# Weight sums one every second step over four chunks, Fourier weights requested by ACT's queue, last residuals in tiles of their own, first position a step later

## The chip, the cores and the metric

The kernel runs on one core of one Trainium2 chip. The metric is the device time of one execution, in microseconds (us). Each time is the median of several runs.

## The reference

The trunk has two layers over two sequences, a prompt of 2048 tokens and a sample of 512, with 1024 channels. All arithmetic is float32.

```python
def attention_layer(x, g, w_in, w_out, sink, rel_bias):
    h = rmsnorm(x, g)
    z = h @ w_in                                  # q, k, v, gate
    ...
    o = banded_gqa_with_sink(q, k, v, rel_bias, sink)   # |i-j| <= 128, 16 heads, 4 kv heads
    return x + (o * jax.nn.silu(gate)) @ w_out

def fourier_layer(x, g, w_gate, w_out):
    h = rmsnorm(x, g)
    hg = h.astype(jnp.float32).reshape(b, s, N_FGROUPS, FGROUP_CH)   # 4 groups of 256 channels
    f = jnp.fft.fftn(hg, axes=(1, 3), norm="ortho").real             # over positions and group channels
    gate = h @ w_gate
    return x + (f.reshape(b, s, d) * jax.nn.silu(gate)) @ w_out

# y = rmsnorm(fourier_layer(attention_layer(x, ...), ...), final_norm), for the prompt and for the sample
```

## The kernel before

Every matmul runs on float32 operands that are split in a high part (rounded to the type fp32r) and a low part (the rest). `matmul3` (L85) issues three matmuls for a product, high by high, high by low and low by high: these are lines L87, L88 and L89, and most of TensorE's work stands in them.

**Attention phase** (`attention_phase`, L120). The tokens are taken in five chunks of 512 (`CHUNKS`, L37): chunk 0 is the sample, chunks 1 to 4 are the prompt. In a chunk, keys and values come first (`kv_proj`), then a loop of 64 positions and a few more for the lag (L564 on, `for i in range(64 + LAG + AVLAG)`). A position is one head pair `p`, one block of 128 queries `b` and one head `j`. At each position the loop issues

- the scores (`scores`, L383): TensorE L389 into a PSUM bank `spt`; DVE L401 adds the bias and finds the maximum, which releases the bank; ACT L405 takes the exponential; DVE L410 divides;
- three positions later the transposes (`transp`, L413): TensorE L421, ACT L422 casts the high part `pts`, DVE L423 takes the low part;
- two positions after that the products with the values (`av`, L435) and their evacuation (`out_evac`, L440, with GpSimd L450 and L453);
- between these, `fill`: the projections of the next head pair, or in the last eighth the output projection (`out_proj`, L457).

The output projection's `evac` (L474) loads the residual `xr` by SyncE (L479), DVE adds the projection (L480), and SyncE stores the sum to `x1d` (L481), the input of the second layer. The tag "xr" has three buffers. The steps of the last chunk's output projection that do not fit in the loop are returned as `tail` and run at the start of the Fourier phase (L846).

**Weight sums.** The gate product of the Fourier layer is done by a scheme with seven products in place of eight. It needs sums of quarters of `w_gate`: B11, T1, T2, B22, T3, N4 and B21. They are made during the attention phase, and go to DRAM (`sumd`) as high and low parts. `gate_sums(k)` (L502) makes the sums of one of four parts in ten steps: a load of two tiles `w32g`, seven `kept` steps and two steps of GpSimd arithmetic (`sums`, `more`). `fout_parts` (L527) splits the output weights in the same way into `foutd`, eight times a load (`w32f`) and two `kept` steps. A `kept` step is `keep` (L495):

```python
                t = ap.tile([P, 2, 512], F32R, tag="x", bufs=4, name="kept")
                ACT.copy(t[:, 0], src)
                pieces(t[:, 1], src, f32(t[:, 0]), ALU.subtract)
                POOL.dma_start(f32(dst), f32(t))
```

The two GpSimd instructions of `pieces` are L493. Loaded and kept tiles share the tag "x" with four buffers. `EXTRA` gives the steps to the chunks, and L590 to L593 issue one at each of the positions 4 to 27.

**Fourier phase** (`fourier_phase`, L619). The 20 tiles of 128 tokens are taken in ten pairs, 17 and 16 first. For a pair, `norms` (L692, with `norm` L673 and `sumsq` L667) loads the tiles of `x1d` and normalises them; the square of `sumsq` (ACT L670) writes to a junk tile of the tag "xr". `turn` (L695) transposes the tiles: TensorE `trb` L701, ACT `tTb` L703, DVE L704 for the low part. `sums` and `parts` make the sums of the transposed tiles. `z` (L725) is the transform over the channels of a group, and `gates` (L759) the seven products. These are accumulated in the PSUM tiles W, Z and X: first W with B11, then X step 0 with B21, Z with T1, W with T2, X step 1, Z with B22, W with T3, X steps 2 and 3, and W with N4. The weights B11 to N4 are loaded once, by `load_sums` (L816, GpSimd L820), four tiles of 512 KB each; those of B21 are streamed through `more` (L751, SyncE). `hook(i)` runs work between the products: the next pair's transposes, sums and `z`. At each second pair `combine` (L875) takes the four tiles' transforms together and stores them (`gsd`, `evd`, `odd`).

The loop over the tail (L846) issues the norms of the first pair (its tiles are loaded by ACT's queue) after tail steps 2 and 4, and the loads of B11, T1, T2 and B22 after step 5.

Then the transform over the positions: `position` (L907) takes the transforms `gl` of the sample (loaded from `gsd` by `sample`, L1005), casts them to `gs` on ACT (L931) and multiplies with the tables into the PSUM tiles As and Bs; the product with the gates `s2` gives `u`. `split_T` (L648) transposes `u` (`tru`, TensorE L655), and `finish` (L959) does the output projection `fo` with the 16 weight tiles `wo` (from `foutd`, loaded by GpSimd), adds the residual x2 and takes the final norm. The first position, of the sample's tiles 2 and 3, is run inside the last pair's gates, at hook 0; the others follow in `step`.

A framework places the instructions: each engine has one queue in order, semaphores between queues are set by the tiles that instructions share, and a tile of a pool waits until the earlier user of its buffer is done.

Of the kernel before, what the change touches and what calls it, by code (L numbers as in the profile page):

```python
# [18 lines left out]
P = 128  # L19
# [25 lines left out]
def encoder(  # L45
# [64 lines left out]
            (SP if lo_engine else POOL).dma_start(f32(wsd[n]), f32(w))  # L110
        return w[:, 0], w[:, 1]

    stage = []

    def after(ins, anchor):

# [3 lines left out]
    def attention_phase():  # L120

        with ExitStack() as es:
# [334 lines left out]
            def out_proj(c, uTs):  # L457
                tok = CHUNKS[c][0]
                steps = []
                st = {}  # L460

                def mm(half, k):
                    if k == 0:
                        st["ps"] = [bank(f"op{c}_{half}_{i}") for i in range(4)]
                    if k % 2 == 0:
                        st["w"] = load_w(c, 20 + half * 4 + k // 2, f"o{c}_{half}_{k}")
                    hi, lo = st["w"]
                    ws = slice((k % 2) * 512, (k % 2) * 512 + 512)
                    for i in range(4):
                        cs = slice(i * P, (i + 1) * P)  # L470
                        a = (uTs[k][0][:, cs], uTs[k][1][:, cs])
                        matmul3(st["ps"][i], a, (hi[:, ws], lo[:, ws]), k == 0, k == KD - 1)

                def evac(half):  # L474
                    for i in range(4):
                        rows = slice(tok + i * P, tok + (i + 1) * P)
                        cols = slice(half * 512, half * 512 + 512)
                        xt = main.tile([P, 512], F32, tag="xr", bufs=3, name=f"xr{c}_{half}_{i}")
                        SP.dma_start(xt, x[rows, cols])  # L479
                        DVE.tensor_tensor(xt, xt, st["ps"][i], ALU.add)  # L480
                        SP.dma_start(x1d[rows, cols], xt)  # L481

                for half in range(2):
                    for k in range(KD):
                        steps.append(lambda half=half, k=k: mm(half, k))
                    steps.append(lambda half=half: evac(half))
                return steps
# [36 lines left out]
                return [load, kept("B11", "B11"), kept("B22", "B22"), kept("B21", "B21"), sums, kept("T3", "B22"),  # L524
                        kept("T1", "B12"), more, kept("T2", "B11"), kept("N4", "B21")]

            def fout_parts(half, k2):  # L527
                st = []

                def load():  # L530
                    st.append(ap.tile([P, 2, 512], F32, tag="x", bufs=4, name=f"w32f{half}_{k2}"))
                    after(SP.dma_start(st[0].rearrange("p k c -> p (k c)"), w_fout[half, k2]), last_exp[0])

                return [load] + [lambda kk=kk: keep(foutd[half * 8 + k2 * 2 + kk], st[0][:, kk]) for kk in range(2)]

            EXTRA = {1: [gate_sums(0), gate_sums(1)], 2: [gate_sums(2), gate_sums(3)],
                     3: [fout_parts(h, k2) for h in range(2) for k2 in range(4)]}

            HB = [(b, j) for b in range(4) for j in range(2)]
            tail = []  # L540
# [6 lines left out]
            for c in range(len(CHUNKS)):  # L547
# [19 lines left out]
                for i in range(64 + LAG + AVLAG):  # L567
                    p, n = divmod(i, 8)
                    if n == 0 and i < 64:
                        if p < 7:  # L570

                            fill = qg_proj(c, p + 1, hs, res[p + 1], invb0)
                            fill.pop(0)()
                            at[p + 1][0]()
                            if i == 0 and c == 0:

                                for s in fill[:8]:
                                    s()
                                fill = fill[8:]
                        else:  # L580
                            op = out_proj(c, uTs)
                            fill, rest, tail = op[:4], op[4:7], op[7:]
                    if c + 1 < len(CHUNKS):
                        if i == 24:
                            norm_steps = stats(c + 1)
                        if i >= 28 and i % 4 == 0 and norm_steps:
                            inv = norm_steps.pop(0)()
                        elif i == 56:
                            invb = spread(c + 1, inv)
                    if i == 3:  # L590
                        extra = [s for steps in EXTRA.get(c, []) for s in steps]
                    if 4 <= i < 28 and extra:
                        extra.pop(0)()  # L593
                    if c == 0 and i % 8 == 3 and 1 <= p < 7:
                        load_w(0, LATE[p - 1], f"late{p}", late=last_exp[0])
                    if i < 64:
                        at[p][1](*HB[n])
                    k = i - LAG
                    if 0 <= k < 64:
                        at[k // 8][2](*HB[k % 8])  # L600
                    if i < 64:
                        m = len(fill) * (n + 1) // 8 - len(fill) * n // 8
                        todo = fill[len(fill) * n // 8 :][:m]
                        for s in todo[: m // 2]:
                            s()
                    k -= AVLAG
                    if 0 <= k < 64 and k % 2 == 1:
                        b = k % 8 // 2
                        at[k // 8][3](b)
                        if b % 2 == 1:  # L610
                            at[k // 8][4](b)
                    if i < 64:
                        for s in todo[m // 2 :]:
                            s()
                    elif rest:
                        rest.pop(0)()
            return tail

    def fourier_phase(tail):  # L619
        with ExitStack() as es:  # L620
# [1 line left out]
            psum2 = es.enter_context(tc.tile_pool(name="psum2", bufs=2, space=PSUM, reuse_waits="tile"))  # L622

            gb = fp.tile([P, D], F32, tag="gb", bufs=1, name="g1b")
            SP.dma_start(gb, bass.AP(g1.tensor, g1.offset, [[0, P], [1, D]]))
            mir = fp.tile([P, 8], I32, name="mir")
            SP.dma_start(mir, mirror)


            def left(shape, dtype, name):  # L630
# [35 lines left out]

            def sumsq(src, name):  # L667
                ss = main.tile([P, 8], F32, tag="ss", bufs=2, name=f"ss{name}")
                junk = main.tile([P, 512], F32, tag="xr", bufs=3, name=f"jk{name}").bitcast(BF16)
                ACT.activation(junk, src, AF.Square, accum_out=ss[:, 0:1])  # L670
                return inv_rms(ss, 1, f"inv{name}")

            def norm(t, queue=SP):  # L673

                xt = left([P, D], F32, f"x1_{t}")
                queue.dma_start(xt, x1d[t * P : (t + 1) * P, :])
                inv = sumsq(xt, f"b{t}")
                DVE.scalar_tensor_tensor(xt, xt, inv[:, 0:1], gb, ALU.mult, ALU.mult)
                return xt

# [4 lines left out]
            class Pair:  # L687
# [1 line left out]
                    self.n, self.ts, self.x, self.ps, self.A, self.F, self.S = n, ts, [None, None], {}, {}, {}, {}  # L689
                    self.zs = [None, None]  # L690

                def norms(self, i, queue=SP):  # L692
                    self.x[i] = norm(self.ts[i], queue)

                def turn(self, i, hf):  # L695

# [119 lines left out]
            def load_sums(place, *names):  # L816
                for w in names:
                    for k in range(4):
                        t = place([P, 2, 512], F32R, f"w{w}_{k}")
                        POOL.dma_start(f32(t), f32(sumd[w][k]))  # L820
                        wg[w][k] = (t[:, 0], t[:, 1])

            def tt(out, a, b, op):
# [21 lines left out]
            pairs = [Pair(2 * gi + i // 2, tiles[i : i + 2]) for gi, tiles in enumerate(order) for i in (0, 2)]  # L845
            for i, s in enumerate(tail):  # L846
                s()
                if i in (2, 4):
                    pairs[0].norms((4 - i) // 2, ACT)
                if i == 5:  # L850
                    load_sums(left, "B11", "T1", "T2", "B22")
            wstack.close()
            zp = es.enter_context(tc.tile_pool(name="zp", bufs=1, side="right", reuse_waits="tile"))

# [37 lines left out]
            for n, pr in enumerate(pairs[:-1]):  # L892
                nx = pairs[n + 1]
                for i in range(2):
                    nx.norms(1 - i)
                gates(pr, {
                    1: [lambda: turns1(nx)], 2: [lambda: turns2(nx)], 3: [lambda: turns3(nx)], 4: [lambda: turns4(nx)],
                    5: [lambda: nx.z(1, 0), lambda: nx.z(1, 1)],
                    6: [lambda: nx.z(0, 0), lambda: nx.z(0, 1), lambda: combine(nx)],
                })  # L900
# [58 lines left out]
            def finish(uT, r, last=False):  # L959
# [2 lines left out]
                out = rows(dst, (r0 - off, r[1]))  # L962
                if last:
                    ss = main.tile([P, 8], F32, tag="ss", bufs=2, name="ssl")
                    junk = main.tile([P, 512], F32, tag="xr", bufs=3, name="jkl").bitcast(BF16)
                x2 = x_tile(f"x2_{r0}")
                SP.dma_start(x2, rows(x1d, r))
                for half in range(2):
# [36 lines left out]
            def sample(k1, ids):  # L1005
                gl = []
                for i in ids:
                    g = zt(f"gl{i}")
                    SP.dma_start(g, gsd[i])
                    gl.append(g)  # L1010
                return f"s{k1}", 4 * k1, gl[0], gl[1] if len(gl) > 1 else None, pair(k1, 4, SEQ)

            first = []
            gates(pairs[-1], {0: [lambda: first.extend(position(*sample(1, (2, 3))))]})
            wo = []
            for k in range(16):
                t = left([P, 2, 512], F32R, f"wo{k}")
# [171 lines left out]
```

## Time and profile before

| | |
|---|---|
| Median of 3 runs | 1752.29 us (1750.26 to 1753.46) |
| Profiled execution | 1751.27 us |
| Its span in the profile | 1749.5 us |
| Mean granted TensorE clock | 0.985 |
| TensorE busy | 1667.1 us, 95% of the span |
| DVE, ACT, GpSimd busy | 1190.6, 857.7, 440.9 us |
| Bytes moved by DMA | 380.35 MB, 217 GB/s in the mean |

The profile is one execution. A line such as "PE spt L389 <- DVE S L401" in the chain of waits says that TensorE's instruction of line L389, which writes tile `spt`, waited for DVE's instruction of line L401 on tile `S`; the numbers behind it are the us in total, the number of waits and the longest one. In the profile PE is TensorE, POOL is GpSimd and SP is SyncE; "kept<-w32g" is an instruction that reads `w32g` and writes `kept`. The granted clock is the share of full speed that TensorE was allowed. The stages in the trace: chunk 0 ends at about 245 us, chunk 1 at 490, chunk 2 at 735, chunk 3 at 950, chunk 4 at 1183; the gates run to 1473 and the positions and the output projection to the end.

### The profile page before, as it was taken

To read this page: it belongs to the slowest core of one execution; us is meant where nothing else is said; L and a number is where in the kernel's file an instruction comes from. 1 tells how busy PE (TensorE), PEld (TensorE's weight loads), DVE (VectorE), ACT (ScalarE), POOL (GpSimd) and SP (SyncE) were. 2 spreads that over 40 slices of the span, in tenths; PEclk is the share of its full clock that TensorE was granted. 3 is DMA by queue.
4 is the path that set the end of the run, shared out by engine and by line. 5 is a ranking of instruction groups with operands and counts; after the bars stand their busy time and mean duration, and the time that the engine had idled before them with its cause. 6 is when DMAs were issued, how large, how long until landed. Compare 5 with 4: busy or idle time off the path is not lost. (4 is left out here: it accounts for less than half of the span.)

```text
span 1749.5 us, 25848 instructions
## 1 busy us (share of the span) xinstructions
PE 1667.1 (95%) x8980; PEld 1422.5 (81%) x8980; DVE 1190.6 (68%) x2774; ACT 857.7 (49%) x1966; POOL 440.9 (25%) x599
## 2 busy tenths in 40 slices
PE   9999899899989899999999999998999998999998
PEld 6878678688887788887888888887888887788886
DVE  5898654788538887457785388835777665888553
ACT  6678533576325575236664166624555543343221
POOL 2467732721305511305313011121000001112000
PEclk9999999899999999999999999998999999999999
DMA  8477776655576554668644843378665559763431
GB/s 303 173 285 302 271 282 234 228 181 196 183 258 244 211 193 148 222 253 283 236 171 164 315 139 125 129 272 353 223 223 181 191 194 405 281 234 111 146 106 49
DMA packets 104638, 380.35 MB, mean 217 GB/s; under 512 B 12171, under 2 KB 22411, under 8 KB 86588
## 3 DMA queue, kind: packets, MB, share of 16 engines
q1 hardware_dynamic: 84924, 294.54, 47.8%
q0 software_dynamic: 19152, 82.85, 12.0%
q8 instruction: 72, 1.18, 0.3%
q10 hardware_dynamic: 432, 1.31, 0.2%
q14 instruction: 58, 0.48, 0.1%
HBM read 284.25 MB, written 94.40 MB: 216 GB/s over the span
## 5 line engine op out<-in xcount | busy, mean ns | idle before, releaser
L405 ACT ACTIVATE S<-S 128x385 f32<-128x385 f32 (+1 forms) x320 | 191.1, 597 | 79.1 <-DVE S L401 78.4
L423 DVE TENSOR_TENSOR pts<-pt,pts 128x384 fp32r<-128x384 f32 (+1 forms) x320 | 168.4, 526 | 48.8 <-ACT pts L422 46.8
L389 PE MATMUL spt<-kwin,qab 128*128 128x384 f32 (+1 forms) x640 | 162.5, 336 | 31.7 <-DVE S L401 31.5
L401 DVE CUSTOM_DVE_ANT_0 S<-spt,b 128x385 f32<-128x385 f32 (+1 forms) x320 | 168.4, 527 | 28.0 <-PE spt L389 24.0
L410 DVE TENSOR_SCALAR S<-S 128x384 f32<-128x384 f32 (+1 forms) x320 | 174.1, 544 | 8.9
L422 ACT CAST pts<-pt 128x384 fp32r<-128x384 f32 (+1 forms) x320 | 143.8, 451 | 71.5 <-PE pt L421 68.2
L389 PEld LDWEIGHTS spt<-kwin,qab 128*128 128x128 f32 x640 | 117.3, 190 | 67.9 <-DVE S L401 44.2
L450 POOL TENSOR_TENSOR o<-o,s 128x256 f32<-128x256 f32 x75 | 55.2, 736 | 416.1 <-DVE o L446 409.7
L421 PE MATMUL pt<-ident,S 128*128 128x128 f32 x896 | 151.5, 275 | 1.4 <-ACT S L405 0.8
L435 PEld LDWEIGHTS av<-pts,v 128*128 128x128 f32 x896 | 128.4, 192 | 15.4 <-DVE pts L423 3.0
L435 PE MATMUL av<-pts,v 128*128 128x256 f32 x896 | 137.3, 287 | 2.3 <-DVE pts L423 2.2
L87 PE MATMUL gp<-h,wg 128*128 128x512 f32 x320 | 139.2, 435 | 0.0
L87 PE MATMUL qp<-h,wq 128*128 128x512 f32 x320 | 137.3, 429 | 0.6 <-ACT wq L101 0.6
L87 PE MATMUL op<-wo,uT 128*128 128x512 f32 x320 | 126.8, 399 | 2.9 <-DVE xr L480 2.8
L421 PEld LDWEIGHTS pt<-ident,S 128*128 128x128 f32 x896 | 114.5, 141 | 17.8 <-DVE pts L423 4.3
L89 PE MATMUL gp<-h,wg 128*128 128x512 f32 x320 | 127.1, 397 | 0.0
L87 PE MATMUL fo<-wo,tTu 128*128 128x512 f32 x320 | 125.9, 393 | 1.2 <-DVE x L973 1.2
L88 PE MATMUL gp<-h,wg 128*128 128x512 f32 x320 | 126.8, 396 | 0.0
L89 PE MATMUL qp<-h,wq 128*128 128x512 f32 x320 | 126.2, 394 | 0.1
L88 PE MATMUL op<-wo,uT 128*128 128x512 f32 x320 | 126.1, 394 | 0.0
L88 PE MATMUL qp<-h,wq 128*128 128x512 f32 x320 | 125.6, 393 | 0.0
L89 PE MATMUL op<-wo,uT 128*128 128x512 f32 x320 | 125.4, 394 | 0.0
(326 smaller groups left out, 4133.5 us busy)
## 6 DMA issues: line engine op xcount, KB each, us to landing
wq<-wsd SPq DMA_DIRECT2D x32, 1024.0 KB, 4.9
wg<-wsd SPq DMA_DIRECT2D x32, 1024.0 KB, 6.8
wo<-wsd SPq DMA_DIRECT2D x32, 1024.0 KB, 4.8
b<-B21d SPq DMA_DIRECT2D x40, 512.0 KB, 5.0
x<-x1d SPq DMA_DIRECT2D x38, 512.0 KB, 4.3
b<-rowd SPq DMA_DIRECT2D x40, 384.0 KB, 4.4
xs<-in_x_dram SPq DMA_DIRECT2D x23, 512.0 KB, 7.1
xr<-in_x_dram SPq DMA_DIRECT2D x40, 256.0 KB, 5.7
```

Source lines behind the costliest of these rows:

```text
L87: PE.matmul(out, a[0], b[0], start=start, stop=False, skip_group_check=more)
L88: PE.matmul(out, a[0], b[1], start=False, stop=False, skip_group_check=more)
L89: PE.matmul(out, a[1], b[0], start=False, stop=stop, skip_group_check=more)
L389: PE.matmul(ps[:, 2 + k0 * P : 2 + k1 * P], q, kwin[g][:, part, b * P + k0 * P : b * P + k1 * P], start=part == 0, stop=part == 1,)
L401: DVE.tensor_tensor_reduce(out=s[:, e0:e1], in0=ps[:, 1 + e0 : 1 + e1], in1=st["bias"][:, j, 386 - e1 : 386 - e0][:, ::-1], scale=1.0, sca ...
L405: last_exp[0] = ACT.activation(s[:, e0:e1], s[:, e0:e1], AF.Exp, bias=mn, scale=-1.0, accum_out=den)
L410: DVE.tensor_scalar(s[:, ks], s[:, ks], den, None, ALU.mult)
L421: PE.transpose(ps[:, kb, :], s[:, 1 + kb * P : 1 + (kb + 1) * P], ident)
L422: ACT.copy(hi[:, k0:k1, j, :], ps[:, k0:k1, :])
L423: DVE.tensor_tensor(lo[:, k0:k1, j, :], ps[:, k0:k1, :], f32(hi[:, k0:k1, j, :]), ALU.subtract)
L435: PE.matmul(out, v, pt[:, kb].rearrange("p h q -> p (h q)"), start=kb == k0 and part == 0, stop=kb == k1 - 1 and part == 1,)
L450: eng.tensor_tensor(of, of, res["s"][:, cs], ALU.mult)
```

## The change

It has six edits.

1. `EXTRA` gives one `gate_sums` to each of chunks 1 to 4, and the fout parts follow the last of them in chunk 4. A step is issued at each even position from 4 on, up to 27 (up to 59 in chunk 4). `fout_parts` loads the next tile with each first part.
2. The loads of B11 to N4 are issued by ACT in place of GpSimd, those of B11 and T1 after tail step 1, those of T2 and B22 after step 4.
3. The loads of the first pair's tiles and of `g1b` are issued after tail step 1, by ACT, apart from the norms. For the other pairs each load still stands right before its norm.
4. The residual tiles `xr` of the tail's last `evac` are allocated apart, each in a place of its own (`res_tile`).
5. The junk tile of the squares takes the tag "c12" (one buffer, shared with the gates' `c12`) in place of "xr". The load of `mir` moves from the start of the Fourier phase to the point before the last gates, on GpSimd.
6. The first position's `gl` tiles are allocated as `x_tile` and requested before the last gates, and the position runs at hook 4 in place of hook 0.

```diff
-    stage = []
+    stage, res_tile = [], []
 ...
-                        xt = main.tile([P, 512], F32, tag="xr", bufs=3, name=f"xr{c}_{half}_{i}")
+                        if res_tile:
+                            xt = res_tile[0](f"xr{c}_{half}_{i}")
+                        else:
+                            xt = main.tile([P, 512], F32, tag="xr", bufs=3, name=f"xr{c}_{half}_{i}")
 ...
-            def fout_parts(half, k2):
+            def fout_parts():
                 st = []
                 def load():
-                    st.append(ap.tile([P, 2, 512], F32, tag="x", bufs=4, name=f"w32f{half}_{k2}"))
-                    after(SP.dma_start(st[0].rearrange("p k c -> p (k c)"), w_fout[half, k2]), last_exp[0])
-                return [load] + [lambda kk=kk: keep(foutd[half * 8 + k2 * 2 + kk], st[0][:, kk]) for kk in range(2)]
-            EXTRA = {1: [gate_sums(0), gate_sums(1)], 2: [gate_sums(2), gate_sums(3)],
-                     3: [fout_parts(h, k2) for h in range(2) for k2 in range(4)]}
+                    n = len(st)
+                    if n < 8:
+                        st.append(ap.tile([P, 2, 512], F32, tag="x", bufs=4, name=f"w32f{n}"))
+                        dst = st[n].rearrange("p k c -> p (k c)")
+                        after(SP.dma_start(dst, w_fout[n // 4, n % 4]), last_exp[0])
+                def part(n, kk):
+                    if kk == 0:
+                        load()
+                    keep(foutd[n * 2 + kk], st[n][:, kk])
+                return [load] + [lambda n=n, kk=kk: part(n, kk) for n in range(8) for kk in range(2)]
+            EXTRA = {1: gate_sums(0), 2: gate_sums(1), 3: gate_sums(2), 4: gate_sums(3) + fout_parts()}
 ...
-                    if i == 3:
-                        extra = [s for steps in EXTRA.get(c, []) for s in steps]
-                    if 4 <= i < 28 and extra:
-                        extra.pop(0)()
+                    if 4 <= i < (60 if c == 4 else 28) and i % 2 == 0 and EXTRA.get(c):
+                        EXTRA[c].pop(0)()
 ...
             gb = fp.tile([P, D], F32, tag="gb", bufs=1, name="g1b")
-            SP.dma_start(gb, bass.AP(g1.tensor, g1.offset, [[0, P], [1, D]]))
             mir = fp.tile([P, 8], I32, name="mir")
-            SP.dma_start(mir, mirror)
 ...
-                junk = main.tile([P, 512], F32, tag="xr", bufs=3, name=f"jk{name}").bitcast(BF16)
+                junk = fp.tile([P, 512], F32, tag="c12", bufs=1, name=f"jk{name}").bitcast(BF16)
 ...
-                        POOL.dma_start(f32(t), f32(sumd[w][k]))
+                        ACT.dma_start(f32(t), f32(sumd[w][k]))
 ...
             for i, s in enumerate(tail):
                 s()
+                if i == 1:
+                    res_tile.append(lambda name: left([P, 512], F32, name))
+                    for k in range(2):
+                        pairs[0].load(1 - k, ACT)
+                    ACT.dma_start(gb, bass.AP(g1.tensor, g1.offset, [[0, P], [1, D]]))
+                    load_sums(left, "B11", "T1")
                 if i in (2, 4):
-                    pairs[0].norms((4 - i) // 2, ACT)
-                if i == 5:
-                    load_sums(left, "B11", "T1", "T2", "B22")
+                    pairs[0].norms((4 - i) // 2)
+                if i == 4:
+                    load_sums(left, "T2", "B22")
 ...
                 for i in range(2):
+                    nx.load(1 - i)
                     nx.norms(1 - i)
 ...
                 for i in ids:
-                    g = zt(f"gl{i}")
+                    g = x_tile(f"gl{i}")
                     SP.dma_start(g, gsd[i])
 ...
+            POOL.dma_start(mir, mirror)
             first = []
-            gates(pairs[-1], {0: [lambda: first.extend(position(*sample(1, (2, 3))))]})
+            one = sample(1, (2, 3))
+            gates(pairs[-1], {4: [lambda: first.extend(position(*one))]})
```

## The prediction

> **What bounds the kernel now.** I read the page's busy times first, then what TensorE waits for, then those waits window by window.
>
> ```profile
> PE 1667.1 (95%) x8980; PEld 1422.5 (81%) x8980; DVE 1190.6 (68%) x2774; ACT 857.7 (49%) x1966; POOL 440.9 (25%) x599
> ```
>
> TensorE is the bound: 1749.5 - 1667.1 = 82 us without matmul is all that better scheduling can win. The chain of waits, for TensorE:
>
> ```profile
> PE spt L389 <- DVE S L401: 31.5, 20, 3.5
> PE As L87 <- ACT gs L931: 7.7, 1, 7.7
> PE z L87 <- DVE xr L480: 7.6, 1, 7.6
> ```
>
> So 46.8 us of the 82 are three kinds of wait: scores waiting for a PSUM bank that L401 still reads, one wait before the first Fourier position, one at the start of the Fourier phase. The windows (columns: window, length, busy us of PE, PEld, DVE, ACT, POOL with counts, granted clock, DMA share, GB/s) give the place and the clock that each wait costs afterwards:
>
> ```profile
> 294.00:326.00 32.00, 27.84 (x149) 23.37 (x149) 26.68 (x64) 18.61 (x46) 22.64 (x33) 0.95 0.71 253
> 326.00:352.00 26.00, 20.76 (x105) 17.48 (x104) 17.77 (x46) 13.66 (x35) 19.96 (x30) 0.87 0.58 206
> 542.00:568.00 26.00, 22.69 (x124) 18.40 (x123) 22.97 (x49) 14.82 (x36) 18.41 (x27) 1.00 0.73 257
> 568.00:594.00 26.00, 20.29 (x95) 16.54 (x94) 20.78 (x44) 13.58 (x33) 21.32 (x32) 0.87 0.59 218
> 798.00:846.00 48.00, 42.58 (x237) 35.17 (x236) 34.30 (x99) 30.60 (x76) 26.79 (x40) 1.00 0.78 277
> 950.00:1147.00 197.00, 197.00 (x1106) 172.10 (x1105) 139.30 (x409) 101.15 (x258) 26.62 (x32) 1.00 0.51 178
> 1187.00:1196.00 9.00, 1.39 (x7) 0.92 (x6) 1.31 (x3) 0.03 (x1) 2.64 (x5) 0.70 1.03 415
> 1196.00:1201.00 5.00, 5.00 (x25) 5.00 (x25) 4.41 (x7) 2.83 (x5) 1.05 (x2) 0.51 1.03 419
> 1463.00:1468.00 5.00, 5.00 (x20) 4.48 (x20) 3.43 (x8) 2.80 (x9) 1.05 (x2) 0.59 1.03 421
> ```
>
> The first five rows are the four weight-sum sets (two in chunk 1, two in chunk 2) and the fout parts (chunk 3). Chunk 4, the sixth row, has no such steps and no idle TensorE. What the sums do is seen in the timelines of ACT, DVE and GpSimd (start, duration, idle before and its releaser):
>
> ```profile
> 335.52 0.62 ACT L498 CAST kept<-w32g 128x512 fp32r<-128x512 f32 x1 [4.68 <-DMA B11d<-kept]
> 1168.86 0.57 POOL L82 TENSOR_TENSOR invb<-invb,mhalf 128x1 f32<-128x1 f32 x1 [12.44 <-DMA mir<-in_mirror_dram]
> 1194.65 0.69 DVE L480 TENSOR_TENSOR xr<-xr,op 128x512 f32<-128x512 f32 x1 [7.96 <-DMA xr<-in_x_dram]
> 1462.04 1.66 ACT L931 CAST gs<-gl 128x512 fp32r<-128x512 f32 x3 [11.79 <-DMA gl<-gsd]
> ```
>
> At 335.52 the `kept` copy is the head of ACT's queue and waits until an earlier kept store frees one of the four "x" tiles. The exp and the pts cast behind it wait too, then DVE, then the scores. That is the mechanism of the 31.5 us.
>
> **Part 1, the weight sums.** Idle plus clock loss ((1 - clock) x length) per set: 4.2 + 1.6 = 5.8; 5.2 + 3.4 = 8.6; 3.3 + 0; 5.7 + 3.4 = 9.1; fout parts 5.4. Sum 32.2 us. The work itself stays: 44 kept copies (28 of w32g, 16 of w32f) at 0.62 us on ACT, their 88 pieces at 0.74 us on GpSimd, 44 stores.
>
> The source says one step every second position. The instruction order that both kernels are built to says otherwise for a set: in chunk 1 ACT has the seven kept copies between the same exps before and after, about one per position. So I don't count the halved pace as a gain for the sets. What does change is that a set no longer follows another directly, finding its "x" tiles still held: the second sets (8.6 and 9.1) are the dear ones, the first sets cost 5.8 and 3.3. After, there are four first sets: 5.8 in chunk 1, 3.3 in chunk 2, and for chunks 3 and 4 the mean, 4.5 each: 18.1. The fout parts do spread: in chunk 4 their copies come as a pair every four positions, with the load one step ahead. Before, they came at about twice that pace and cost 5.4. I take 1.5, nearer to zero since chunk 4 had 197.00 of 197.00 busy and carries no next chunk's norms. After: 19.6. **Gain 32.2 - 19.6 = 13 us.** Ends: the chunk 3 and 4 steps are free (9.1 left: gain 23), or each set costs today's mean of 6.7 and fout stays at 5.4 (32.2: gain 0).
>
> The granted clock weighs here: in 294:326 the longest single wait is 2.6 us and the clock still fell to 0.95, so I charge clock to shorter waits as well. The Trainium skill ("TensorE: Matmul & The Clock Gate", Part 1: The HAM clock gate) says that the clock halves after at least one idle window of about 3.4 us; by it first sets would cost idle alone, 1.6 us less in chunk 1; the trace disagrees for this one.
>
> **Part 2, the start of the Fourier phase.** Before, TensorE waits 7.61 us (to 1195.39) and then runs 5.5 us at half clock (2.7 lost): 10.4 us. The chain: the residual load xr4_1_3 is issued at 1187.75, when the store of the tile whose buffer it takes over has landed; it lands at 1194.57; DVE's L480 waits for it with the transposed tiles' parts queued behind; z17_1 waits for those. GpSimd issues B11_0 and B11_1 at 1155.4, is then held by invb until 1169.4, and issues the rest until 1197.8.
>
> After, the residuals have tiles of their own, so that wait is gone, but another stands in its place: in the built order SP's and ACT's transfers share eight completion lanes, each issue waiting for the transfer eight earlier, and the four xr4_1 loads wait for T2_0 to T2_3 to land. ACT issues g1b, two x1 tiles, then 16 weight tiles, 512 KB each, from about 1161.5. DMA is saturated from 1165 (1.03, 415 GB/s): 0.524 MB take 1.26 us. Up to T2_3 that is 15 tiles, 19 us, plus the last attention weights and stores: landed at about 1183 to 1188, so xr4_1_3 lands at about 1190 to 1194, sharing with B22. z17_1 starts at about 1193 instead of 1195.4.
>
> Behind it: T3_0 and T3_1 on ACT wait for B22_0 and B22_3 (about 1191 and 1196), and tTb16, which z16 needs, is queued behind T3_1. All z of the pair now precede W0, so no W covers the wait, as it did before (L87 W at 1186.24). X0 needs b21_0, which landed at 1208.7 before and can't be sooner: the bytes are the same and DMA is full until 1210. So I expect about 6 idle at z17_1, 3 at z16, 1 later, and 2.4 of clock: 12.4. **Loss 2 us.** Ends: -10 (all waits covered) and +8 (z16 at 1203).
>
> The 24 requests leave GpSimd (0.53 us each) for ACT (0.33 to 0.6 each, by the few ACT issues there are); the first 11, about 5 us, lie in a stretch where ACT is busy 2.1 to 2.5 us of each window of 7 to 15. What moving them wins is the 13.5 us in which GpSimd was held, and DMA's slack in 1150:1165, share 0.79, that is 3 us. The Trainium skill ("Trainium Kernel Development and Optimization", Key Constraints) says that requests from several queues run on the same 16 DMA engines and save only issue time; the share of 1.03 agrees, and without that rule the end of -10 would be nearer.
>
> **Part 3, the gates.** From 1210 to 1450 TensorE has no gap over 0.5 us. The junk tile of sumsq now shares the single c12 buffer, so each square waits for the gate product that reads c12, and the next c12 copy for it; ACT and DVE have room. I take 0; ends -1 and +4 (eight norms at 0.5).
>
> **Part 4, the first position.** Before, its second gl load sat in SP's queue behind the odd and evd stores (issued at 1451.07, gs copied at 1462.04). TensorE idles 7.7 us from 1455.02, then runs 4.4 us at half clock (the 0.59 row): 9.9 us. After, both gl loads are issued before the last gates and the position runs at hook 4, four products later; this wait goes. What is late next: the 16 wo tiles, requested by GpSimd, landed from 1448.1 to 1479.5 with DMA at 1.02 and more, then s2s (1487.1) and x2 (1489.6). fo began at 1474.18; it would now be ready at about 1465, when wo7 (1465.7) has just landed, and its second half needs wo15. The gl loads (1 MB, 2.5 us) are out of that stretch. I return 4 of 9.9. **Gain 6 us;** ends 0 (wo sets the end) and 10.
>
> **The rest**, 1500 to 1749: the built order barely moves; 0.
>
> **Sum.** -13 + 2 + 0 - 6 = -17 us. The profiled run took 1751.27 (span 1749.5 and 1.8 around it): 1734.3. The median is 1.0 above that run: **1735 us.**
>
> **Rivals.**
> (a) *The sums' stalls only move* (the edit doesn't do what it says): the order of copies in a set is unchanged, which speaks for it; that second sets are dearest speaks against. Part 1 gains 0: 1752.3 - 4 = 1748.
> (b) *The sums become free in chunks 3 and 4*, which the full sixth row speaks for: part 1 gains 23: 1752.3 - 27 = 1725.
> (c) *Slower: ACT's queue at the Fourier start.* The evacuations tTb, s1, S1 stand behind weight requests whose lanes wait for landings at a full DMA. If each link (z17_1, z16, X0, the next pair's transposes) waits for a landing, TensorE idles from 1186.4 to about 1208 but for some 10 us of z and W at half clock (5 lost), and the next pair's x1_19, requested after T3_0 landed, adds 10: 12 + 5 + 10 = 27 against 10.4, and SP's b21 stream behind it keeps the gates short of weights for another 8: loss 25, and 1752.3 - 19 + 25 = 1758. It decides from a loss of 19 on, that is when z16_0 starts after about 1205. For it: the lanes in the order; against it: half of ACT's requests go out before TensorE needs anything.
> (d) *wo sets the end*: part 4 gains nothing: 1741.
>
> **How the numbers follow.** Forecast with (d), 1728 to 1744: 0.54. (a): 0.15. (b): 0.13. (c) and its neighbours: 0.18. I leave out about 1 in 10 on each side: 1720 to 1757. A measurement of this kernel tells 0.2%, 3.5 us, from no change (runs 1750.26 to 1753.46). Faster: 0.54 + 0.13 + most of (a), 0.07 = 0.74. Same: 0.08. Slower: 0.18.
>
> **What would show it.** Right: L389's wait for L401 at 18 to 20 us, no such waits behind 330 in chunk 1 and 570 in chunk 2, under 3 in the fout stretch of chunk 4; z17_1 at about 1193 less what came earlier; L87 As without wait, fo waiting for wo or x2. Wrong: kept copies waiting for stores as long as now in chunks 3 and 4; tTb16 behind T3 for over 10 us; z or X waits of over 20 us in all before the second pair.

## The result, and the profile after

The changed kernel takes 1770.55 us (median of 4 runs, 1768.63 to 1773.79), the kernel before 1752.88 beside it: ratio 1.0104, interval 1.0083 to 1.0125. It is slower by 17.7 us where 17 us of gain were forecast. The profiled span is 1767.8 us against 1749.5.

The busy times and the chain of waits for TensorE, after:

```profile
PE 1673.8 (95%) x8980; PEld 1424.1 (81%) x8980; DVE 1194.9 (68%) x2774; ACT 862.3 (49%) x1966; POOL 425.8 (24%) x576
PE spt L389 <- DVE S L401: 29.9, 20, 2.9
PE trb L708 <- DVE xr L483: 11.9, 2, 10.9
PE X L87 <- DMA b<-B21d: 11.3, 2, 5.7
PE tru L662 <- DVE us L970: 3.1, 2, 1.9
```

The two single waits of before, z for xr and As for gs, are gone as planned. In their places stand trb waiting for an xr addition and X waiting for B21. The scores' wait has hardly moved in sum; it has moved in place. Windows after (columns as before):

```profile
294.00:326.00 32.00, 27.83 (x149) 23.32 (x148) 26.60 (x64) 18.47 (x46) 22.66 (x33) 0.95 0.55 219
326.00:352.00 26.00, 26.00 (x153) 22.84 (x152) 22.36 (x73) 16.57 (x44) 4.44 (x6) 1.00 0.49 171
1040.00:1130.00 90.00, 81.70 (x431) 67.65 (x431) 67.44 (x192) 54.77 (x139) 44.02 (x64) 0.94 0.72 251
1182.00:1194.00 12.00, 1.07 (x9) 0.83 (x8) 1.38 (x2) 1.66 (x3) 0.00 (x0) 0.62 1.01 376
1211.00:1217.00 6.00, 0.34 (x2) 0.31 (x2) 1.59 (x3) 4.39 (x9) 0.55 (x1) 0.88 1.03 421
1471.00:1478.00 7.00, 1.39 (x8) 1.08 (x7) 1.92 (x5) 1.62 (x6) 1.54 (x3) 0.78 1.03 417
```

The first set of chunk 1 costs what it did, the place of the second set is full (26.00 of 26.00), and the fout stretch of chunk 4 (1040 to 1130) now has 8.3 us idle and a clock of 0.94. The other three rows are the start of the phase and the end of the gates.

The span cut at instructions that both traces have gives the account. "Start" runs from the last op to the second pair's W, "last gates" from the last pair's W to the end of the gates. The eight pairs between take 213.0 us in every run, 213.2 in two.

| us | to chunk 4's keys | keys to op | op | start | last gates | to the last fo | to the end |
|---|---|---|---|---|---|---|---|
| before | 972.1 | 158.1 | 52.9 | 44.4 | 31.5 | 270.1 | 7.4 |
| after | 949.0 | 179.0 | 53.9 | 58.8 | 30.1 | 271.6 | 12.5 |
| difference | -23.1 | +20.9 | +1.0 | +14.5 | -1.4 | +1.5 | +5.1 |

Chunks 1 to 3 gain 23, chunk 4 gives nearly all of it back, the start loses 14.5, the first position wins nothing, and the last stretch, which no step of the prediction looked at, loses 5.1. That stretch ends with GpSimd's last long drain (the instruction DRAIN). The instructions of the program's last line (count, then least/median/most ns), before and after:

```profile
L1184 POOLq DRAIN  x3: 46/97/2870, 1744.1 to 1749.2; - x3
L1200 POOLq DRAIN  x3: 46/97/9653, 1757.4 to 1767.5; - x3
```

In the kernel before the longest of the three ended at 1747.0, and SyncE's last waits only at 1748.7. After, it ended at 1767.0, with SyncE done at 1762.0. So of the drain's 6.8 us more, 5.1 show.

### The profile page after: what moved, and what is told of

Read it like the earlier page. It is cut to its first block, busy times and chain, and to the rows that moved or that the text cites. A ratio compares the mean times of both kernels' runs of the same rounds, so it can differ in the third digit from the quotient of the medians.

```text
span 1767.8 us, 25793 instructions
## 1 busy us (share of the span) xinstructions
PE 1673.8 (95%) x8980; PEld 1424.1 (81%) x8980; DVE 1194.9 (68%) x2774; ACT 862.3 (49%) x1966; POOL 425.8 (24%) x576
## 5 line engine op out<-in xcount | busy, mean ns | idle before, releaser
L410 DVE TENSOR_SCALAR S<-S 128x384 f32<-128x384 f32 (+1 forms) x320 | 167.8, 525 | 9.1
```

The lines of the kernel that those rows point to most:

```text
L410: DVE.tensor_scalar(s[:, ks], s[:, ks], den, None, ALU.mult)
```

## The experiments

The same cut is used for all. The stretch before chunk 4 differs by 5.6 us between runs of the same code (971.9 to 977.5), so the later stretches are read by themselves. Ratios are to the kernel before, run beside each.

| us | to keys 4 | keys to op | op | start | last gates | to last fo | to end | ratio (interval) |
|---|---|---|---|---|---|---|---|---|
| e1 sums alone | 948.9 | 179.1 | 53.8 | 44.0 | 31.4 | 270.2 | 7.4 | 0.9988 (0.9974-1.0003) |
| e2 start alone | 974.2 | 158.1 | 52.8 | 57.0 | 32.2 | 269.6 | 12.5 | 1.0101 (1.0085-1.0118) |
| e3 position alone | 973.5 | 158.1 | 52.9 | 44.3 | 28.6 | 274.5 | 7.4 | 1.0009 (0.9995-1.0024) |
| e4 after, GpSimd loads | 949.9 | 179.5 | 54.8 | 52.2 | 29.7 | 271.9 | 7.5 | 1.0049 (1.0033-1.0066) |
| e5 no prefetch | 948.4 | 171.2 | 54.4 | 44.3 | 31.3 | 271.7 | 7.4 | 0.9955 (0.9939-0.9970) |
| e6 pinned | 942.9 | 166.6 | 54.0 | 44.0 | 31.6 | 269.8 | 7.4 | 0.9877 (0.9856-0.9897) |
| e7 B21 first | 973.4 | 158.1 | 52.9 | 44.6 | 22.2 | 280.3 | 7.4 | 0.9999 (0.9986-1.0012) |
| e8 24 requests more | 951.3 | 178.5 | 53.9 | 81.3 | 29.8 | 272.8 | 7.5 | 1.0185 (1.0159-1.0210) |
| e9 ACT queue alone | 977.5 | 158.1 | 52.9 | 53.1 | 31.0 | 271.6 | 12.4 | 1.0068 (1.0048-1.0087) |
| e10 own tiles alone | 971.9 | 158.1 | 52.9 | 50.9 | 31.8 | 270.6 | 7.4 | 1.0052 (1.0035-1.0069) |
| e11 pinned, no prefetch | 942.4 | 170.4 | 55.1 | 43.6 | 31.6 | 271.9 | 7.4 | 0.9922 (0.9902-0.9941) |
| e12 after, GpSimd, late | 953.7 | 178.8 | 53.9 | 50.4 | 29.2 | 273.6 | 7.5 | 1.0037 (1.0022-1.0052) |
| e13 X late | 944.6 | 166.8 | 54.0 | 46.9 | 32.1 | 269.9 | 7.4 | 0.9918 (0.9893-0.9944) |
| e14 pinned alone | 970.8 | 158.1 | 52.9 | 43.8 | 31.3 | 270.8 | 7.4 | 0.9965 (0.9950-0.9979) |
| e15 122 requests | 951.4 | 178.2 | 53.8 | 52.2 | 29.0 | 272.0 | 7.4 | one run, 1759.28 us |

**e1: the sums alone** (edit 1 on the kernel before).

> The kernel before with edit 1 alone (the weight sums spread over four chunks, fout parts in chunk 4). Theory: the trace of after shows chunk 4's keys starting 23.1 us sooner and chunk 4's output projection starting only 2.2 us sooner, so the edit gives back in chunk 4 what it won: from before, -2 us in all (-5 to +1), L389 waits in chunk 4 about 8 us in the fout stretch, with half clock three times. Rival (my forecast): the loss in chunk 4 comes with the other edits, and alone this one gains 13 us.

-1.7 us in the spans, the ratio near 1. Chunk 4's loss belongs to the sums; my forecast of 13 us falls.

**e2: the start alone** (edits 2 to 5).

> The kernel before with edits 2 to 5 alone (weights by ACT's queue, early first tiles, residuals in tiles of their own, junk in c12's buffer). Theory: these cost what the trace of after shows between the end of the last op and the second pair's W, +14 us (12 to 17), with about 11 us of waiting for a bank at the transposes trb and about 6 us of X waiting for B21. Rival (the forecast): +2 us, and the rest came from chunk 4's late weight sums, whose stores would still be in the DMA queues when the phase starts.

The start is 57.0, +12.6, with waits of 10.0 us at trb and 6.1 at X: the first theory. At most the 1.8 us between its start and that of after (58.8) can come over from chunk 4. The last 5.1 us belong to these edits too.

**e3: the position alone** (edit 6).

> The kernel before with edit 6 alone (gl requested before the last gates, first position at hook 4). Theory: the wait of 7.7 us for gs goes, and X waits for the last B21 tile in its place, since that load stands behind the odd and evd stores: -1.5 us (-3 to 0), an X wait of about 5.6 us near the end of the gates. Rival (the forecast): -6 us, because without the other edits the last B21 tile lands before X needs it.

The last gates win 2.9 and the stretch behind them loses 4.4; the rival falls. X waited 4.6 us for B21, as the theory said; its -1.5 us can't be told from none (the interval reaches from 0.9 us faster to 4.2 slower).

**e4: the weights by GpSimd again.**

```diff
-                        ACT.dma_start(f32(t), f32(sumd[w][k]))
+                        POOL.dma_start(f32(t), f32(sumd[w][k]))
```

> The kernel after with the loads of B11 to N4 issued by GpSimd again; all else as in after. Theory A (ACT's queue and the completion lanes that it shares with SyncE make the start late): the wait at trb falls from 10.9 to under 5 us and the kernel is 8 to 14 us faster than after. Theory B (the early requests fill DMA, whoever issues them, and push the last residuals back): within 3 us of after, the trb wait stays near 11 us. The last GpSimd drain, 9.7 us in after and 2.9 in before, is watched: if it goes with the number of GpSimd requests (110 in after, 133 in before), it falls back to about 3.

The span is 9.4 us shorter than after's (1758.4), the wait at trb falls to 2.2 us and the drain is back at 2.96: theory A's numbers. But the start is still 52.2, for X now waits 13.2 us for B21:

```profile
PE X L87 <- DMA b<-B21d: 13.2, 1, 13.2
PE trb L708 <- DVE xr L483: 2.2, 1, 2.2
```

Theory B's mechanism, the early weights pushing back what SyncE needs, may stand behind A's; e12 tests that.

**e5 and e6: why the sums cost.** e5 loads each fout tile in a step of its own and issues at two of three positions from 24 on. e6 holds the copies to their places by an anchor, an order dependency on the last exp issued:

```diff
-                ACT.copy(t[:, 0], src)
+                after(ACT.copy(t[:, 0], src), last_exp[0])
```

> e1 (sums alone) without the fout load one step ahead: each tile is loaded by a step of its own before its two kept steps; the fout steps go at two of three positions, so the pace of the pairs is the same, one in about 4.5 positions. Theory (buffers): with the next tile loaded ahead, two of the four x tiles are loads and each kept copy waits for the store of the pair before; without it these waits (10.9 us on ACT in five copies) go, L389's 8 us behind them too and the half clock after them: chunk 4 from keys to output projection 179.1 -> 167 us (164 to 170), 12 us faster than e1. Rival (the stores' own landing, 8 to 9 us beside the loads, or the copies' 0.6 us themselves): 176 us or more.

> e1 with every kept copy held behind the last exp that the source had issued by then, so that ACT's queue has the copies one every second position, as the change says; in after a set's seven copies stand at seven successive positions. Theory (pace): a set's copies then find the store of two copies before landed; the set's waits (3 to 6 us idle and 1.7 of clock a chunk in chunks 1 to 4) fall to under 1 us, 10 to 15 us faster than e1. Rival (a set's cost is ACT's and GpSimd's work itself): within 3 us of e1. Between: chunk 4's fout stretch, still with two loads held, keeps its 8 us and more.

ACT's timeline shows the fault in after, and TensorE's chain of waits from 1040 to 1130 what it costs there:

```profile
1065.43 0.62 ACT L501 CAST kept<-w32f 128x512 fp32r<-128x512 f32 x1 [2.49 <-DMA foutd<-kept]
1089.55 0.62 ACT L501 CAST kept<-w32f 128x512 fp32r<-128x512 f32 x1 [3.29 <-DMA foutd<-kept]
```
```profile
PE spt L389 <- DVE S L401: 8.2, 4, 2.9
```

and the chain of waits for ACT in the fout stretch, after first, then e5, then e6:

```profile
ACT kept L501 <- DMA foutd<-kept: 10.9, 5, 3.3
```
```profile
ACT kept L498 <- DMA w32f<-in_w_fout_dram: 8.0, 4, 3.8
```
```profile
ACT kept L498 <- DMA foutd<-kept: 3.5, 3, 1.6
ACT kept L498 <- DMA w32f<-in_w_fout_dram: 0.6, 1, 0.6
```

Without the prefetch the wait for the stores is gone, as the theory of the buffers says, but a wait for the load itself takes most of its place: 171.2, between the two. Held to every second position, with the prefetch, both nearly go. The anchor does what was meant: in e6's trace the copies stand two positions apart or more, in after a set's seven copies come about one a position and the fout copies mostly in pairs every four. The windows of e6 over the first set of chunk 1 and the fout stretch:

```profile
294.00:326.00 32.00, 30.86 (x175) 26.16 (x174) 25.67 (x77) 19.82 (x51) 18.53 (x27) 1.00 0.51 176
1025.00:1109.00 84.00, 79.90 (x449) 67.44 (x448) 67.33 (x204) 56.27 (x147) 44.44 (x65) 1.00 0.79 267
```

Full clock in both; 1.1 us idle in the first where after had 4.2. From e1 to e6 the keys of chunks 1 and 4 lie 5.0 us closer together, the first 25 positions of chunk 4, with its set, are 3.4 us shorter, and positions 25 to 58, with the fout parts, 8.9: about half comes from the sets' order and half from the fout parts'. e6 takes 1734.62 us, 1.2% less than before. It is faster than both kernels, with one line more than the sums' edit.

**e11: both together; e14: the anchor on the kernel before**, with one step at every position and two sets a chunk.

> e6 (copies held to their positions) with e5's fout loads (none ahead). If pace and buffers are two causes, chunk 4 from keys to output projection falls below both (166.6 in e6, 171.2 in e5; 158.1 without any steps): 160 to 164 us, and the kernel is 3 to 6 us faster than e6. If the pace alone is the cause, it is within 1.5 us of e6.

> The kernel before with the kept copies held behind the last exp and nothing else: two sets in chunks 1 and 2, fout parts in chunk 3, one step at every position. Theory (pace: a copy needs about two positions for the store two copies before it): no gain, -3 to +5 us, since the copies still come one a position. Rival (the anchor alone helps, by keeping the copies from being moved ahead): -8 us or more.

e11 is slower than e6 in chunk 4 (170.4 against 166.6): the loads of their own come with a pace of two in three positions, and together they cost more than the buffer returns. Neither theory had that. ACT waits 8.1 us in four copies for these loads, as in e5 (8.0), and for no store; how much the pace adds was not separated. In e14 the spans differ by 1.4 us and the ratio says 0.35%, 6 us: a little more than expected, a fraction of e6. In 280:360 its copies still wait 8.0 us for stores, where e6's don't wait at all. The anchor needs the room of every second position.

**e9: ACT's queue alone** (e4's line the other way round, on the kernel before).

> The kernel before with one word changed: load_sums issues on ACT in place of GpSimd, at its old place after tail step 5. Theory (queue): in e4 the queue alone was worth 6.7 us of the start and 5.1 us of the last drain, so here the stretch from the last op to the second pair's W grows by 4 to 10 us (44.4 before) and the last drain goes from 2.9 to 9.7 us, since GpSimd has about 109 requests: before + 12 us (8 to 16). Rival (the queue hurts only when the requests come early, as in after): start within 2 us of before, + 5 us by the drain alone.

Start +8.7 and a drain of 9.57 us, as the theory said. A lane is one of the eight completion semaphores that SyncE's and ACT's requests take in turn; a request waits until the one that took its lane before has landed. ACT's timeline in its start, and TensorE's chain of waits:

```profile
1187.60 5.70 ACTq L820 DMA_DIRECT2D wT<-T2d  x4
1194.26 6.18 ACTq L820 DMA_DIRECT2D wB<-B22d  x4
1200.48 1.56 ACT L703 CAST tTb<-trb 128x512 fp32r<-128x512 f32 x3 [22.16 <-DMA wB<-B22d]
```
```profile
PE z L87 <- ACT tTb L703: 10.5, 1, 10.5
```

Four requests take ACT 5.7 and 6.2 us, most of it waiting for lanes (four B22 requests took 1.9 us in after), and the cast that z wants is queued behind the last of them: ACT computes nothing for 22 us.

**e10: the residuals' own tiles alone; e12: e4 with the weights after tail step 5.**

> The kernel before with edit 4 alone (last residuals in tiles of their own). Theory A (buffers made z wait 7.6 us): the four loads go out early, that wait and its half clock go, -5 to -10 us in the start. Theory B (DMA is full from 1165 to 1210 and X needs its B21 tile whatever comes before): the wait for xr goes, but X waits for B21 in its place; start 40 to 44 us, gain 0 to 4 us. Theory C (the completion lanes tie SyncE's loads to earlier transfers): no gain, or a loss of up to 5.

> e4 (after, weights by GpSimd) with all of B11, T1, T2 and B22 requested after tail step 5, as in before. e4's start took 52.2 us against 44.4, with 13.2 us of X waiting for B21. Theory (early requests of the weights put everything that SyncE needs behind them on a full DMA): start back to 44 to 46 us. Rival (the order of the products, with X in its natural place, makes X wait, whenever the weights come): 50 us or more.

e10, chain of waits for TensorE in the start:

```profile
PE X L87 <- DMA b<-B21d: 10.7, 1, 10.7
PE trb L704 <- DVE xr L483: 2.2, 1, 2.2
```

z's wait for xr is gone, 2.2 us are left at trb, and the start is 6.6 us longer: worse than all three theories. The built order changed. In before W (T2), Z (B22) and most of W (T3) stand ahead of the first X step; with the xr wait away, X's first step stands right behind Z (T1), and b21_0 holds up products whose weights had landed. e12 says the same: requesting the weights late does little (50.4 against e4's 52.2), and X still waits 10.4 us.

The B21 tile was also requested late. SyncE's own wait in e10, from 1183 to 1215:

```profile
SPq L679 <- DMA x1d<-xr: 10.2, 1, 10.2
```

The load of the next pair's tile stood 10.2 us until a store to `x1d` had landed, and b21_0 was requested behind it, at 1199.7. In e4 and e12 the same wait is 10.7 and 10.0 us. No run requested B21 ahead of that load, so how much of X's wait is the full DMA and how much this order is open.

**e13: e6 with the own tiles and X late.**

```diff
-                x_step(0)
+                if n:
+                    x_step(0)
...
+                for k in () if n else range(3):
+                    x_step(k)
                 hook(4)
```

> e6 (the fastest so far) with edit 4's own residual tiles and, in the first pair alone, the first three X steps after the product with T3 and the next pair's transposes one hook later. In e10 the own tiles made the start 50.9 us in place of 44.4, because X waited 10.7 us for B21 with products behind it whose weights had landed. Theory (X's place in TensorE's queue): the start comes to 40 to 46 us. Rival (DMA is full and the last weights set the end, whatever the order): 49 us or more.

46.9, between the theory and its rival: X's place, with the transposes moved along, was worth 4 of the 6.6 us, and the rest is another transfer, in ACT's chain of waits in the start and then TensorE's:

```profile
ACT jkb L679 <- DMA x<-x1d: 7.8, 1, 7.8
```
```profile
PE W L87 <- ACT c L795: 7.4, 1, 7.4
```

The square of the next pair's tile waits for its load, with the copy of W behind it. In these runs each wait taken away gave the next one. No version of the start was faster than before's.

**e7: the last B21 tiles ahead of the radix-4 stores.**

```diff
-                    6: [lambda: nx.z(0, 0), lambda: nx.z(0, 1), lambda: combine(nx)],
+                    6: [lambda: nx.z(0, 0), lambda: nx.z(0, 1)] + [more] * (2 if n == 8 else 0) + [lambda: combine(nx)],
```

> e3 (position alone) with the last two B21 tiles requested before the last radix-4 stores instead of behind them. Theory A (SyncE's queue): X's 4.6 us of waiting at the end of the gates go, and the kernel gains 3 to 6 us over e3. Theory B (DMA is full from 1450 to 1500 and sets the end, whatever stands first): the X wait goes but the same time comes back before the first fo or in the positions: within 1.5 us of e3.

Theory B. The last gates take 22.2 in place of e3's 28.6 and the next stretch 280.3 in place of 274.5; fo and As, which did not wait so in e3, now do:

```profile
PE fo L87 <- DMA wo<-foutd: 4.0, 3, 1.5
PE As L87 <- DMA tbs<-in_tabs_dram: 1.9, 1, 1.9
```

**e8 and e15: the last drain.** e8 adds 24 small GpSimd requests at the start of the phase, e15 adds 12.

> The kernel after with 24 more GpSimd requests of 4 KB each at the start of the Fourier phase (134 in all in place of 110; their data is not used). Theory A: the last GpSimd drain is long (9.65 us in after and e2, both with 110 requests) or short (2.87 to 2.96 with 133 or 134) by the number of its requests: it falls to about 3 us and the kernel is 4 to 6 us faster than after. Theory B: it goes with the weights' bytes or packets on GpSimd's ring, or with ACT's use of its own ring: it stays at 9.65.

> The kernel after with 12 small GpSimd requests behind the wo loads: 122 in all. If the last drain's length goes with the number of requests since some number at which the queue was cleared, it is 10.6 us (0.088 us each, 122 of them) or, if the clearing comes before 122, under 3 us. If it stays at 9.65 us, it doesn't go with their number in this range.

```profile
L1203 POOLq DRAIN  x3: 46/97/2958, 1782.6 to 1787.8; - x3
```
```profile
L1203 POOLq DRAIN  x3: 46/97/1977, 1751.7 to 1756.8; - x3
```

The drain goes with the number of requests, not with their bytes: 109 give 9.57 us, 110 give 9.65, 122 give 1.98, 133 give 2.87 and 134 give 2.96. In e8 the requests, each waiting for the one before to land, held GpSimd's queue ahead of the norms: TensorE waited 20.6 and 7.2 us at trb for them, more than the 22.5 by which its start (81.3) is longer than after's. In e15 the builder spread the 12 requests over the start (1153 to 1206), which is 52.2 against 58.8 in after with the same edits: so the 6.7 us of e4 can't be put down to the queue alone. e9 can, since its wait is seen.

## Why the prediction was wrong, point by point

**Part 1** forecast -13 and got -1.3 (-23.1 + 20.9 + 1.0). That second sets are the dear ones held: between the keys of chunks 1 and 4 23.5 us were gained where the sum had 18.6. The step that failed is the price of the fout parts in chunk 4, "I take 1.5, nearer to zero since chunk 4 had 197.00 of 197.00 busy": idle-free is not the same as having room, for what counts is ACT's queue in order, and a copy at its head that waits 3 us stops the scores whatever TensorE did before. The fout stretch cost 8.3 idle and 0.06 x 90 = 5.4 of clock, 13.7 in place of 1.5. The prediction noted the load one step ahead and not that it takes one of four buffers. It also saw that a set's order was unchanged and took that as given; e6 shows that the order of the copies, the sets' and the fout parts', was the main thing left to win.

**Clock.** The rows 294:326 (0.95) and 1040:1130 (0.94, longest wait 2.9 us) bear out charging clock to waits under 3 us: in the second, waits of 1.9, 2.9 and 2.2 us were each followed by 3.4 us at half clock. For these the Trainium skill ("TensorE: Matmul & The Clock Gate", Part 1: The HAM clock gate), which names an idle window of about 3.4 us, would have charged nothing.

**Part 2** forecast +2 and got +14.5. Rival (c) named the right queue, with a loss below the 25 of its price: in 1182:1200 ACT's casts and a copy stood 6.8, 5.4 and 4.9 us behind its requests. But TensorE's long wait came at none of (c)'s links. The step that failed is "about 6 idle at z17_1": TensorE did not get that far.

```profile
1185.06 4.05 SPq L482 DMA_DIRECT2D xr<-in_x_dram  x4
1192.88 0.69 DVE L483 TENSOR_TENSOR xr<-xr,op 128x512 f32<-128x512 f32 x1 [6.17 <-DMA xr<-in_x_dram]
1193.62 1.11 PE L708 MATMUL trb<-ident,x 128*128 128x128 f32 x4 [10.93 <-DVE xr L483]
```

trb's third bank is one that op had filled, released by the xr addition; that load was issued at 1185 and landed at 1192.9, so TensorE stopped at trb for 10.9 us. The four loads did wait for T2's landings, 10.7 us in all, as the prediction said; but the last, xr4_1_3, landed at 1198.0, outside the 1190 to 1194. "1 later" failed too: X waited 5.7 for B21, whose first tile was requested at 1206.4 and landed at 1216.6, where the kernel before had 1198.9 and 1208.7. The Trainium skill ("Trainium Kernel Development and Optimization", Key Constraints) says that another issuing engine saves only the sequencer's issue time. e9 agrees: DMA moved 378 and 392 GB/s in 1180:1190 and 1190:1200, the kernel before 417 and 415. What e9 shows beside that is the other side, 22 us of ACT's casts standing behind its own requests.

**Part 3** was right: 213.0 us in both. No run had the junk tile's move by itself.

**Part 4** forecast -6 and got 0.1 (-1.4 + 1.5). The step that failed is "I return 4 of 9.9": all of it came back. Rival (d)'s number was right, partly by luck, since the wait did not go to wo but where neither looked, to the last B21 tile behind the radix-4 stores (5.6 us at X in after, 4.6 in e3). wo stands second: with that wait gone, in e7, fo waits for it.

**The rest**, "1500 to 1749: 0", missed the drain: +5.1. Moving 24 requests was costed at the queue that gets them and the time that GpSimd is held, not at the end of the program.

Errors of 11.3, 12.5, 6.1 and 5.1 us make 35.0, from -16.6 (part 1 is 12.6 before rounding) to +18.4, against 18.3 in the spans.

## What to carry to other kernels

Work in the gaps of a tight loop is priced by the wait of its own first instruction: count buffers against the time that a store takes to land, and check in the built order whether the builder keeps the spacing that the source writes; one anchor turned this change's sums from -2 to -20 us. Where DMA was full, taking away one wait showed the next, so add up the bytes that must land before each product and look at the built order before costing the gain. A queue that also carries the casts on the path is no place for requests that wait for lanes.

## What the runs showed of the hardware that was not expected

GpSimd's last drain lengthens by about 0.08 us a request ((2.96 - 1.98) / 12 from 122 to 134 requests; 9.65 / 110 = 0.088) and drops by some 9 us between 110 and 122 requests. That the queue's finished requests are cleared at some count would fit; it was not shown. And the start of the phase took 52.2 us with 12 requests of 4 KB more (e15), 58.8 and 57.0 (after, e2) without. Each is from one profiled run, and why the start was shorter with them is open.
